# A decoder trunk on one core: how the mixer's GpSimd pieces of weights become a high and a low part

## The chip, the core and the metric

The kernel runs on one core of a Trainium2 chip. A core has five engines with a queue each: TensorE (PE in the profile, with its weight loads as PEld), VectorE (DVE), ScalarE (ACT), GpSimd (POOL) and SyncE (SP), which here only issues transfers. Sixteen DMA engines move the data, whichever queue issues them. The metric is the device time of one execution in microseconds (us). Three runs of the kernel before gave 1470.0, 1470.25 and 1474.0 us; the median is 1470.25.

## The reference

Two layers work on 256 tokens of 1024 features in float32. Each layer is a feed-forward block, a token mixer and a second feed-forward block, each with an RMS norm before and after it:

```
f = swiglu_ffn(rmsnorm(x, ffn1_norm_pre), ffn1_w_in, ffn1_w_out);  x = x + 0.5 * rmsnorm(f, ffn1_norm_post)
h = rmsnorm(x, mix_norm_pre);  p = h @ mix_w_in
qkv, z, beta_logit, a_logit, glu_in, gates = split(p)
y_a = gated_deltanet(qkv, z, beta_logit, a_logit, ...)      # causal convolution of 4 taps, delta rule in chunks
y_b = conformer_conv(glu_in, ...)                           # gated linear unit, causal convolution of 31 taps
g_a, g_b = split(sigmoid(gates));  y = (g_a * y_a + g_b * y_b) @ mix_w_out
x = x + rmsnorm(y, mix_norm_post)
f = swiglu_ffn(rmsnorm(x, ffn2_norm_pre), ffn2_w_in, ffn2_w_out);  x = x + 0.5 * rmsnorm(f, ffn2_norm_post)
```

The feed-forward blocks are 1024 x 5632 and 2816 x 1024 matrices; the mixer's input matrix is 1024 x 8208, and three of 1024 x 1024 follow it.

## The kernel before

All matrices are read once, in the order of use, as 444 pieces of 128 x 1024 float32 (512 KB; eight of them are 128 x 544). To keep float32 accuracy, each piece becomes two: a high part `hi`, the piece rounded to TensorE's float32r type, and a low part `lo`, exactly the rest. Activations are split in the same way, and a product is taken as three (`mm3`, lines 363 to 365): high x high, high x low, low x high.

`Stream` makes the pieces. `load_one` (lines 132 to 147) takes a raw buffer (three of them), and a high and a low buffer of a ring of `RING = 8` each. SP issues the load into the raw buffer (line 138), ScalarE copies it with rounding into `hi` (line 146), and VectorE or GpSimd subtracts `hi` from the raw piece into `lo` (line 147). `done()` is called when a piece's last product has been emitted; it emits the load of the next piece but seven, which can use the ring slot when TensorE has finished with it.

The list `side` says which engine subtracts: VectorE for all 66 + 66 pieces of the feed-forward blocks of a layer, GpSimd for the mixer's pieces 3, 16 to 63 and 67 out of 90 (`POOL`, line 64). With two layers that is 100 pieces for GpSimd and 344 for VectorE.

In the mixer, pieces 0 to 65 are the input matrix in 17 column chunks (`PLAN`), pieces 66 to 89 the three square matrices. A chunk's sums go into PSUM, are scaled by ScalarE (line 893), transposed by TensorE (line 509), and worked on by VectorE and ScalarE: convolutions of 4 taps (`c`, line 558) and of 31 taps (`cacc`, line 542), the decays of the delta rule (`decays`, lines 580 to 630), the inverses of 32 x 32 blocks (`iu`, lines 710 and 712, 31 steps of a product and a subtraction), and Newton steps for inverse square roots (`nw_a`, `nw_y`, lines 242 to 252).

The order of the work is set in two ways. On TensorE instructions are issued in the order in which the code emits them; `Lanes` puts transposes and small products between the big ones after a number of ticks written by hand (`DELAY`). On the other engines a planner orders the instructions by readiness in its own reckoning and by priority, which is program order with offsets (`CFG`). GpSimd has, beside the subtractions, one multiplication of `ktok` for each head group (line 666) and memsets of `u` (line 676) and `at` (line 744).

Of the kernel before, what the change touches and what calls it, by code (L numbers as in the profile page):

```python
# [9 lines left out]
F32 = mybir.dt.float32  # L10
# [3 lines left out]
ALU = mybir.AluOpType  # L14

P = 128
D = 1024
# [9 lines left out]

# columns of the per-channel parameter table
C_CW, C_DW, C_DB, C_BA, C_BG, C_LG, C_LB, C_NW = 0, 96, 344, 352, 360, 368, 376, 384
N_PCH = 385  # L30
# rows of the per-feature parameter table
R_F1PRE, R_F1POST, R_MPRE, R_MPOST, R_BO, R_F2PRE, R_F2POST = range(7)
# columns of the constants
K_ID, K_TRI, K_ONE, K_MASK = (128 * i for i in range(4))


# The mixer's column chunks in their order, each with the work that follows it; "f" takes its own sums.
PLAN = [
# [4 lines left out]
]  # L43
# Work between the products goes in steps: ticks (of three products) before each of them.
DELAY = {
# [7 lines left out]
}  # L53
# what has to be done before a piece of work starts
AFTER = {
# [6 lines left out]
}  # L62
# what has to be done when a chunk's sums are taken
BEFORE = {"z0": ("qt0",), "z1": ("qt1",), "b0": ("merge",), "b1": ("merge",), "a0": ("qt0",), "a1": ("qt1",)}
# the mixer's pieces whose split is GpSimd's
POOL = {3, *range(16, 64), 67}
# offsets of priority against program order
CFG = dict(stat=0, conv=-800, ev=1000, tok=4, st=4, post=300, pre=100, fin=None, tokens=200)


class Lanes:
    """Work in steps, between the products."""

# [43 lines left out]
class Stream:  # L117
    """Weights in the order of use: DRAM -> raw -> (hi, lo), hi + lo == raw exactly."""

# [12 lines left out]
    def load_one(self, parts=1):  # L132
        nc, src = self.nc, self.pieces[self.nload]
        n = src.shape[-1]
        raw = self.pool.tile([P, D], F32, name="raw", tag="raw", bufs=3)
        hi = self.pool.tile([P, D], F32R, name="whi", tag="whi", bufs=RING)
        lo = self.pool.tile([P, D], F32R, name="wlo", tag="wlo", bufs=RING)
        nc.sync.dma_start(raw[:, :n], src)
        eng = nc.gpsimd if self.side[self.nload] else nc.vector
        self.loaded.append((hi, lo))  # L140
        self.nload += 1
        for i in range(parts):
            if i:
                yield
            c = slice(i * n // parts, (i + 1) * n // parts)
            nc.scalar.copy(hi[:, c], raw[:, c])  # L146
            eng.tensor_tensor(lo[:, c], raw[:, c], hi.bitcast(F32)[:, c], op=ALU.subtract)  # L147

# [10 lines left out]
def trunk(ctx: ExitStack, tc: tile.TileContext, x_in, wfirst, consts, feat, pch, tokp,  # L159
# [35 lines left out]

    # ---- the residual stream and constants
    def xtile(tb):
# [39 lines left out]
    def rsqrt(o, v, n):  # L237
        """o = v ** -0.5 by a seed and Newton's steps."""
        y = work.tile([P, n], F32, name="nw_y", tag=f"nw_y{n}", bufs=2)
        a = work.tile([P, n], F32, name="nw_a", tag=f"nw_a{n}", bufs=2)  # L240
        hv = work.tile([P, n], F32, name="nw_h", tag=f"nw_h{n}", bufs=2)
        V.tensor_scalar(y.bitcast(I32), v.bitcast(I32), 1, None, op0=ALU.logical_shift_right)
        V.tensor_scalar(y.bitcast(I32), y.bitcast(I32), -1, 0x5F3759DF, op0=ALU.mult, op1=ALU.add)
        V.tensor_scalar(hv, v, -0.5, None, op0=ALU.mult)
        for it in range(3):
            dst = o if it == 2 else y
            if n == 1:
                V.scalar_tensor_tensor(a, y, y, hv, op0=ALU.mult, op1=ALU.mult)
            else:
                V.tensor_tensor(a, y, y, op=ALU.mult)  # L250
                V.tensor_tensor(a, a, hv, op=ALU.mult)
            V.scalar_tensor_tensor(dst, a, 1.5, y, op0=ALU.add, op1=ALU.mult)

    def split(hi, lo, src):
        """hi + lo == src"""
        S.copy(hi, src)
        V.tensor_tensor(lo, src, hi.bitcast(F32), op=ALU.subtract)  # L257
# [3 lines left out]

    # activations for the products: two tiles of four k-tiles, each with its high and its low parts
    def halves(tb):
        return [slots.tile([P, 2, 4, P], F32R, name="xt", tag=f"xt{tb}{hf}") for hf in range(2)]

    # ---- x * w, transposed and split; the rms of x goes into a per-token scale
    def pre(tb, wbc, xws):
# [24 lines left out]

    # ---- the same for the kernel's input, with w by channels, in step with the first pieces of the weights
    def start():
# [48 lines left out]

    # ---- x += half * rmsnorm(f) * w
    def post(tb, acc, wbc, half, fws, jks):
# [20 lines left out]

    # ---- h @ w for a list of chunks (columns, k-tiles of a piece); ev takes the sums, fin goes on
    def proj_in(xt, chunks, ev, fin, first=2):
# [34 lines left out]

    # ---- act @ w, all 1024 columns at once; the last 8 k-tiles one token block after the other
    def proj_out(lhs, nkt, ev, tails=0, need=None):
# [34 lines left out]

    # ---- feed-forward
    def ffn(xt, l, wpost, after, first=2, tails=0):
# [35 lines left out]

    # ---- token mixing
    def mixer(xt, l, after_mix):  # L480
# [22 lines left out]

        # -- staging of sums: scaled, transposed to channel-major, both token blocks side by side
        def to_channels(stage, cols):
# [5 lines left out]

        # ---- conformer module: gated linear unit
        hT = [slot(0, [P, 4, SEQ], name="hT0"), slot(1, [P, 4, SEQ], name="hT1")]
# [35 lines left out]

        # ---- delta rule  # L550
        ba = small(32, "ba", bufs=1).rearrange("p (k g b h) -> p k g b h", k=2, g=2, b=2)
# [17 lines left out]
        rq = small(16, "rq", bufs=1)  # L569
        ex = small(32, "ex", bufs=1)     # exp of: G | Gend - G  # L570
        neg_eg = small(16, "neg_eg", bufs=1)
# [61 lines left out]

        # sums over the channels of the squares, by tokens
        def squares(src, si):
# [85 lines left out]

        # the inverses of the 32-blocks on the diagonal, put together to 64 and to 128; the lower half of AT
        # and its diagonal blocks take what is in between
        def merge():
# [99 lines left out]

        # the first 128 tokens, from an empty state
        def scan_first():
# [15 lines left out]

        # the other 128
        def scan_second():
# [27 lines left out]

        # ---- the column chunks
        chunks = [{"ka": (272, 2), "kb": (256, 4)}.get(name, (512, 2)) for name, _ in PLAN]
# [175 lines left out]

        # gate[0..1]: tanh of g_a / 2; gate[2..3]: of g_b / 2; sigmoid = (tanh + 1) / 2
        def ev_b(tb, acc):
# [51 lines left out]

    # ---- layers
    xt = [None, None]
# [25 lines left out]
def _pieces(w, cols, kp):  # L1132
    """[L, K, N] -> [L, pieces, 128, kp * len(cols)], kp k-tiles to a piece"""
    s = w[:, :, cols]
    n_l, k, n = s.shape
    return s.reshape(n_l, k // (P * kp), kp, P, n).transpose(0, 1, 3, 2, 4).reshape(n_l, k // (P * kp), P, kp * n)
# [65 lines left out]
```

## Time and profile before

| | |
|---|---|
| time, median of 3 runs | 1470.25 us |
| span of the profiled execution | 1470.4 us |
| TensorE busy | 1395.6 us (95%) |
| VectorE busy | 1059.0 us (72%) |
| ScalarE busy | 769.5 us (52%) |
| GpSimd busy | 249.1 us (17%) |
| moved by DMA | 250.64 MB, mean 170 GB/s |
| mean granted clock of TensorE | 0.976 |

The profiled execution's span, from its first to its last instruction, stands for its time. The profile gives busy time by engine, by line and by stretch of the span. A row of a group reads: line, engine, operation, output <- inputs, shapes, count, then busy time and mean length in ns, then the idle time of the engine just before, and what ended it. A row of waits reads: engine and line, what it waited for, us in total, times, the longest. A row of a timeline reads: start, length, engine, line, operation. A row of DMA issues ends with the size of one and the median us from issue to landing. Neighbouring matmuls overlap, so their starts, not their lengths, give TensorE's pace. The first mixer lies between about 200 and 545 us, the second between about 930 and 1290.

### The profile page before, as it was taken

The numbers are of one execution on the slowest core, as the hardware profiler recorded it, in microseconds if no ns is written. First come the engines' busy times: TensorE is split into PE (matmuls) and PEld (weight loads), VectorE is DVE, ScalarE is ACT, GpSimd is POOL, SyncE is SP. The second block draws the span as 40 slices with busy tenths as digits, with TensorE's granted clock in tenths as the row PEclk, the third lists the DMA queues.
The fourth block names the chain that finished last, engine by engine and source line by source line (L and its number), as shares of the span: only waits on it lengthen the run. The fifth ranks groups of instructions, "written<-read, shape, count | busy, mean of one in ns | idle before, by whom it ended". The sixth has DMA issues, their size and how long they took to land.

```text
span 1470.4 us, 19499 instructions
## 1 busy us (share of the span) xinstructions
PE 1395.6 (95%) x6972; PEld 1154.8 (79%) x6972; DVE 1059.0 (72%) x2095; ACT 769.5 (52%) x1198; POOL 249.1 (17%) x116
## 2 busy tenths in 40 slices
PE   8999999886999999999999999996969999999997
PEld 6788878675778887888878888785758888788886
DVE  6655478899899877655486553898999997875543
ACT  7544357555555646544355443665555664464441
POOL 0000015445550000000000000173556300000000
PEclk9999999799999999999999999997989999999999
DMA  7766546343434556655466565553434435665551
GB/s 253 229 189 186 190 154 202 132 135 115 117 128 138 195 192 198 211 182 180 151 222 214 186 182 162 189 200 103 148 115 138 147 128 189 201 201 186 186 187 57
DMA packets 82962, 250.64 MB, mean 170 GB/s; under 512 B 21136, under 2 KB 21680, under 8 KB 82864
## 3 DMA queue, kind: packets, MB, share of 16 engines
q1 hardware_dynamic: 82576, 249.32, 52.3%
q8 instruction: 55, 0.90, 0.2%
q14 instruction: 43, 0.35, 0.1%
q10 hardware_dynamic: 288, 0.07, 0.0%
HBM read 245.14 MB, written 4.21 MB: 170 GB/s over the span
## 4 chain that ended last, share of the span: by engine, by line
PE 68%; DVE 20%; DMA 5%; ACT 4%; issue 2%; POOL 1%; DVEq 0%; ACTq 0%; POOLq 0%
PE mm L363 20%; PE mm L365 20%; PE mm L364 20%; DVE cacc L542 4%; DVE iu L712 2%; DVE c L558 2%; DVE iu L710 2%; DVE wlo L147 2%; DMA raw<-w1i 2%; ACT whi L146 2%; DMA raw<-mw 1%; PE tr L460 1%; PE gd L645 1%; DVE fw L352 1%; POOL wlo L147 1%
## 5 line engine op out<-in xcount | busy, mean ns | idle before, releaser
L146 ACT CAST whi<-raw 128x1024 fp32r<-128x1024 f32 (+2 forms) x445 | 462.8, 1041 | 382.7 <-PE mm L365 259.6
L147 DVE TENSOR_TENSOR wlo<-raw,whi 128x1024 fp32r<-128x1024 f32 (+2 forms) x345 | 417.3, 1212 | 272.3 <-ACT whi L146 265.3
L363 PE MATMUL mm<-whi,xt 128*128 128x512 f32 (+2 forms) x1280 | 515.9, 403 | 0.9 <-ACT whi L146 0.9
L365 PE MATMUL mm<-whi,xt 128*128 128x512 f32 (+2 forms) x1280 | 501.2, 392 | 3.8 <-DVE xt L257 3.6
L364 PE MATMUL mm<-wlo,xt 128*128 128x512 f32 (+2 forms) x1280 | 499.6, 390 | 0.5 <-DVE wlo L147 0.5
L365 PEld LDWEIGHTS mm<-whi,xt 128*128 128x128 f32 x1280 | 244.5, 191 | 60.1 <-DVE xt L257 7.5
L364 PEld LDWEIGHTS mm<-wlo,xt 128*128 128x128 f32 x1280 | 245.4, 192 | 45.3 <-DVE wlo L147 1.7
L363 PEld LDWEIGHTS mm<-whi,xt 128*128 128x128 f32 x1280 | 245.3, 192 | 45.2 <-ACT whi L146 1.3
L147 POOL TENSOR_TENSOR wlo<-raw,whi 128x1024 fp32r<-128x1024 f32 x100 | 239.7, 2410 | 236.4 <-ACT whi L146 228.1
L542 DVE SCALAR_TENSOR_TENSOR cacc<-hT,pc,cacc 128x254 f32<-128x254 f32 (+28 forms) x464 | 191.4, 462 | 4.9 <-ACT cacc L538 4.9
L363 PE MATMUL mm<-whi,act 128*128 128x512 f32 x352 | 137.6, 391 | 0.0
L365 PE MATMUL mm<-whi,act 128*128 128x512 f32 x352 | 137.1, 389 | 0.0
L364 PE MATMUL mm<-wlo,act 128*128 128x512 f32 x352 | 136.9, 389 | 0.0
L676 POOL MEMSET u<- 128x1024 f32 x4 | 3.8, 960 | 669.6 <-ACT jk L351 647.7
L365 PEld LDWEIGHTS mm<-whi,act 128*128 128x128 f32 x352 | 66.1, 188 | 13.9
L363 PEld LDWEIGHTS mm<-whi,act 128*128 128x128 f32 x352 | 66.1, 188 | 13.5
L364 PEld LDWEIGHTS mm<-wlo,act 128*128 128x128 f32 x352 | 66.1, 188 | 13.4
L448 ACT ACTIVATE ag<-mm,rstd 128x256 f32<-128x256 f32 x88 | 41.1, 474 | 56.8 <-DVE ag L449 23.9
L558 DVE SCALAR_TENSOR_TENSOR c<-tr,pc,c 128x255 f32<-128x255 f32 (+1 forms) x144 | 66.4, 473 | 2.0 <-ACT c L556 1.6
L449 DVE SCALAR_TENSOR_TENSOR ag<-mm,rstd,ag 128x256 f32<-128x256 f32 x88 | 41.6, 480 | 20.4 <-ACT ag L448 20.4
L556 ACT ACTIVATE c<-tr,pc 128x256 f32<-128x256 f32 x48 | 22.3, 472 | 54.6 <-DVE c L558 51.6
L352 DVE SCALAR_TENSOR_TENSOR fw<-mm,wbc 128x512 f32<-128x512 f32 x24 | 16.0, 687 | 46.2 <-ACT jk L351 46.2
(225 smaller groups left out, 1353.8 us busy)
## 6 DMA issues: line engine op xcount, KB each, us to landing
raw<-mw SPq DMA_DIRECT2D x168, 512.0 KB, 3.4
raw<-w1i SPq DMA_DIRECT2D x88, 512.0 KB, 4.0
raw<-w2i SPq DMA_DIRECT2D x88, 512.0 KB, 3.7
raw<-w1o SPq DMA_DIRECT2D x44, 512.0 KB, 3.6
raw<-w2o SPq DMA_DIRECT2D x44, 512.0 KB, 3.4
wbc<-feat SPq DMA_DIRECT2D x13, 512.0 KB, 4.6
raw<-mkb SPq DMA_DIRECT2D x8, 272.0 KB, 3.0
xs<-x SPq DMA_DIRECT2D x4, 512.0 KB, 3.6
```

Of the source, the lines that this page charges most:

```text
L146: nc.scalar.copy(hi[:, c], raw[:, c])
L147: eng.tensor_tensor(lo[:, c], raw[:, c], hi.bitcast(F32)[:, c], op=ALU.subtract)
L352: V.scalar_tensor_tensor(fw[:, cs], acc[hf], half, wbc[:, cs], op0=ALU.mult, op1=ALU.mult)
L363: T.matmul(o, xh, wh, start=start, stop=False)
L364: T.matmul(o, xh, wl, start=False, stop=False)
L365: T.matmul(o, xl, wh, start=False, stop=stop)
L448: S.activation(a[:, 0, :], ps[:, 0:256], AF.Silu, scale=xt[tb][1])
L449: V.scalar_tensor_tensor(a[:, 1, :], ps[:, 256:512], xt[tb][1], a[:, 0, :], op0=ALU.mult, op1=ALU.mult)
L542: cur = V.scalar_tensor_tensor(accs[i][:, sh:], h_of(t)[:, :SEQ - sh], dw(t, KW - 1 - sh), accs[i][:, sh:], op0=ALU.mult, op1=ALU.add)
L558: V.scalar_tensor_tensor(acc[:, sh:], src[:, :SEQ - sh], cw(t, 3 - sh), acc[:, sh:], op0=ALU.mult, op1=ALU.add)
L710: V.tensor_tensor(tmp, u[:, 0:n, s:s + 1].broadcast_to([P, n, m]), a[:, s:s + 1, s + 1:32].broadcast_to([P, n, m]), op=ALU.mult)
L712: V.tensor_tensor(u[:, 0:n, s + 1:32], u[:, 0:n, s + 1:32], tmp, op=ALU.subtract)
```

## The change

For the pieces that `side` gives to GpSimd, `load_one` now takes no raw buffer. GpSimd issues a DMA that reads the float32 piece from DRAM and writes it, cast to float32r, into `hi`. ScalarE multiplies `hi` by -1 into `lo`. GpSimd then issues a second DMA of the same piece from DRAM, which adds it to what stands in `lo`. GpSimd's subtraction is gone; the matrix piece is read twice. VectorE's pieces go as before, and so do the ring, the products and TensorE's order.

```diff
     def load_one(self, parts=1):
         nc, src = self.nc, self.pieces[self.nload]
         n = src.shape[-1]
-        raw = self.pool.tile([P, D], F32, name="raw", tag="raw", bufs=3)
         hi = self.pool.tile([P, D], F32R, name="whi", tag="whi", bufs=RING)
         lo = self.pool.tile([P, D], F32R, name="wlo", tag="wlo", bufs=RING)
-        nc.sync.dma_start(raw[:, :n], src)
-        eng = nc.gpsimd if self.side[self.nload] else nc.vector
+        by_dma = self.side[self.nload]
         self.loaded.append((hi, lo))
         self.nload += 1
+        if by_dma:
+            nc.gpsimd.dma_start(hi[:, :n], src)
+            nc.scalar.mul(lo[:, :n], hi.bitcast(F32)[:, :n], -1.0)
+            nc.gpsimd.dma_start(lo[:, :n], src, accum_op=ALU.add)
+            return
+        raw = self.pool.tile([P, D], F32, name="raw", tag="raw", bufs=3)
+        nc.sync.dma_start(raw[:, :n], src)
         for i in range(parts):
             if i:
                 yield
             c = slice(i * n // parts, (i + 1) * n // parts)
             nc.scalar.copy(hi[:, c], raw[:, c])
-            eng.tensor_tensor(lo[:, c], raw[:, c], hi.bitcast(F32)[:, c], op=ALU.subtract)
+            nc.vector.tensor_tensor(lo[:, c], raw[:, c], hi.bitcast(F32)[:, c], op=ALU.subtract)
```

## The prediction

> **What bounds the kernel now.** I read the page's busy times and its row of granted clock, then the busy times by stretches of 100 us, then the waits of TensorE, and last the groups and single instructions of VectorE and GpSimd in the first mixer.
>
> ```profile
> PE 1395.6 (95%) x6972; PEld 1154.8 (79%) x6972; DVE 1059.0 (72%) x2095; ACT 769.5 (52%) x1198; POOL 249.1 (17%) x116
> ...
> PEclk9999999799999999999999999997989999999999
> ...
> PE 68%; DVE 20%; DMA 5%; ACT 4%; issue 2%; POOL 1%; DVEq 0%; ACTq 0%; POOLq 0%
> ```
>
> ```profile
> 100.00:200.00 100.00, 100.00 (x453) 82.77 (x451) 51.71 (x63) 42.27 (x50) 2.16 (x2) 1.00 0.57 175
> 200.00:300.00 100.00, 86.13 (x450) 72.64 (x447) 84.85 (x231) 63.90 (x106) 41.83 (x20) 0.91 0.50 166
> 300.00:400.00 100.00, 86.35 (x410) 71.40 (x411) 91.75 (x220) 53.45 (x98) 53.59 (x23) 0.92 0.42 129
> ...
> 1000.00:1100.00 100.00, 78.89 (x366) 64.96 (x365) 94.27 (x238) 53.26 (x99) 51.11 (x23) 0.87 0.40 129
> ```
>
> The columns after the length are PE, PEld, DVE, ACT, POOL, granted clock, DMA share and GB/s. In the feed-forward (100 to 200) TensorE is full at clock 1.00. In the mixers it is not: 14 to 21 us of 100 idle, clock down to 0.87, VectorE at 85 to 94. What TensorE waits for there, over the whole run:
>
> ```profile
> PE tr L781 <- ACT vT L560: 17.9, 6, 5.7
> PE tr L509 <- DVE at L686: 10.8, 2, 5.8
> PE tr L509 <- ACT stg L893: 9.3, 7, 3.1
> PE gd L609 <- DVE g L605: 7.0, 2, 3.5
> ```
>
> Together 45.0 us, and none of it is a wait for weights: it is the mixer's own chain, which runs through VectorE. The idle time costs twice, since right after it the clock is low: at full clock the first of these rows (start, length) and the next but one start 0.45 us apart, 0.225 a product; behind a stall two neighbours of the chain of waits start 0.42 apart.
>
> ```profile
> 236.24 0.39 PE L364 MATMUL mm<-wlo,xt 128*128 128x512 f32 x1
> ...
> 236.69 0.39 PE L363 MATMUL mm<-whi,xt 128*128 128x512 f32 x1
> ```
>
> ```profile
> 279.33 0.43 PE mm L363
> 279.75 0.43 PE mm L364
> ```
>
> What the clock took in the three mixer stretches above: 0.09 x 86.1 + 0.08 x 86.4 + 0.13 x 78.9 = 24.9 us. So the most that any relief of the mixers can give is 45.0 + 24.9 = 70 us.
>
> VectorE is late in the mixers because of GpSimd. One subtraction of GpSimd takes 2.4 us, and VectorE's small instructions that start under one end only with it:
>
> ```profile
> L147 POOL TENSOR_TENSOR wlo<-raw,whi 128x1024 fp32r<-128x1024 f32 x100 | 239.7, 2410 | 236.4 <-ACT whi L146 228.1 <-ACT cacc L538 6.2 <-PE gd L732 1.4
> ```
>
> ```profile
> 331.75 7.06 POOL L147 TENSOR_TENSOR wlo<-raw,whi 128x1024 fp32r<-128x1024 f32 x3 [5.43 <-ACT whi L146]
> ```
>
> ```profile
> 331.99 2.28 DVE L710 TENSOR_TENSOR iu<-iu,ia 128x96 f32<-128x96 f32 x1
> ...
> 334.56 2.06 DVE L712 TENSOR_TENSOR iu<-iu 128x96 f32<-128x96 f32 x1
> ...
> 336.94 2.02 DVE L710 TENSOR_TENSOR iu<-iu,ia 128x115 f32<-128x115 f32 x1
> ...
> 339.27 0.26 DVE L712 TENSOR_TENSOR iu<-iu 128x115 f32<-128x115 f32 x1
> ```
>
> GpSimd's three subtractions run from 331.75 to 338.81; the three VectorE instructions under them take 2.0 to 2.3 us, and the next one of the same width, after them, 0.26.
>
> **The change part by part.** The sum is made against the profiled execution, a span of 1470.4 us; that is the runs' median (1470.25) but for 0.2 us, so no correction lies between.
>
> Removed are GpSimd's 100 subtractions, and with them what they hold VectorE up. These groups carry most of it:
>
> ```profile
> L712 DVE TENSOR_TENSOR iu<-iu 128x126 f32<-128x126 f32 (+22 forms) x62 | 40.8, 659 | 0.1
> L710 DVE TENSOR_TENSOR iu<-iu,ia 128x126 f32<-128x126 f32 (+22 forms) x62 | 37.4, 604 | 0.1
> L251 DVE TENSOR_TENSOR nw_a<-nw_a,nw_h 128x8 f32<-128x8 f32 (+1 forms) x30 | 19.2, 643 | 0.3
> L580 DVE TENSOR_TENSOR pre_a<-ba,tp 128x16 f32<-128x16 f32 x2 | 4.7, 2328 | 0.0
> L252 DVE SCALAR_TENSOR_TENSOR rq<-nw_a,nw_y 128x16 f32<-128x16 f32 x2 | 4.3, 2170 | 0.0
> L605 DVE SCALAR_TENSOR_TENSOR g<-lm,aexp 128x16 f32<-128x16 f32 x2 | 4.2, 2110 | 0.0
> L595 DVE TENSOR_TENSOR ls<-ls 128x16 f32<-128x16 f32 x2 | 4.1, 2058 | 0.0
> L599 DVE SCALAR_TENSOR_TENSOR lp<-lp,ls 128x16 f32<-128x16 f32 x14 | 2.3, 163 | 0.0
> ```
>
> L710 and L712 take 78.2 us in 124 instructions; at the free 0.26 us they would take 32.2, so 46.0 are excess. L251 at the free 0.163 us of line 599 (same kind of width) would take 4.9: 14.3 excess. Lines 580, 252, 605 and 595 take 17.3 in 8 instructions against 1.3: 16.0. Together **76 us**, 38 for each mixer, against the 70 that TensorE can give back. These lines are on the chain that makes `g`, the inverse and `vT`, for which TensorE waits; but TensorE's order is fixed in ticks, and some of these waits have several causes. I take half of the ceiling, **35 us** of gain; the ends are 0 and 70.
>
> ScalarE's part is moved, not added: a copy 128x1024 becomes a multiplication by -1 of the same shape, at 1.04 us a piece (462.8 us for 445 pieces). What changes is what it waits for. The copy waits for a free ring slot, with its raw data landed before; the multiplication waits for a landing that itself cannot start before the slot is free.
>
> ```profile
> L146 ACT CAST whi<-raw 128x1024 fp32r<-128x1024 f32 (+2 forms) x445 | 462.8, 1041 | 382.7 <-PE mm L365 259.6
> ```
>
> Added are two transfers of 512 KB a piece, and their issue on GpSimd.
>
> ```profile
> raw<-mw SPq DMA_DIRECT2D x168, 512.0 KB, 3.4
> x<-xs SPq DMA_DIRECT2D x4, 512.0 KB, 5.9
> ```
>
> ```profile
> 212.54 0.33 SPq L487 DMA_DIRECT2D xs<-x  x1
> ```
>
> A plain 512 KB (0.524 MB) lands 3.4 us after its issue. What it costs all 16 engines: in the stretch 100 to 200, 17.5 MB are 33.4 pieces and 57 us of engine time, 1.7 us each. For the casting one I take the same 1.7 and 3.4, since it moves the same bytes (its ends: 3.4, and the 5.9 of the slowest plain 512 KB). No row shows an accumulating transfer. Below it is a plain one, 1.7; above, three passes one after another (read the source, read what stands in the ring, write), 5.1. I take 2.5, nearer to the plain one, because the DRAM side is that of a plain one and the rest stays on the chip. So the engines have 4.2 us of work a piece. A DMA's issue on GpSimd is not in the trace either: between SP's 0.33 and the 2.4 of the subtraction it replaces; I take 0.7, twice SP's.
>
> What the pieces need: GpSimd's first and last low part of the run of 48 pieces (16 to 63) in the first mixer are
>
> ```profile
> 233.42 2.41 POOL L147 TENSOR_TENSOR wlo<-raw,whi 128x1024 fp32r<-128x1024 f32 x1 [19.90 <-ACT whi L146]
> ...
> 437.77 2.40 POOL L147 TENSOR_TENSOR wlo<-raw,whi 128x1024 fp32r<-128x1024 f32 x1 [0.48 <-ACT whi L146]
> ```
>
> 204 us for 47 steps, 4.35 us a piece. At full clock a piece costs TensorE 12 x 0.225 = 2.7 us, so the ring's 7 other pieces cover 19 us. The new way from free slot to low part is 0.7 + 3.4 + 1.04 + 0.7 + 3.4 = 9.2 us where nothing is in its way: covered, with about 10 us to spare. If that cover is gone, each us of it is a us of TensorE.
>
> Now GpSimd's queue. An accumulating DMA waits there for ScalarE's multiplication, and behind it stand the next casting DMA, the four multiplications of `ktok` (L666) and the memsets of the merge (L744). The planner orders GpSimd by when work comes ready in its own reckoning, so I expect casting DMA i+1 ahead of accumulating DMA i: a slot comes free every 2.7 to 4.35 us, a low part is ready for its sum 3.4 + 1.04 later. Then from one accumulating DMA to the next but one: issue 0.7, the transfer of the former 2.5, landing 3.4, ScalarE 1.04, issue 0.7, sum 8.3, 4.2 us a piece. That is under 4.35, and just enough for half the relief (204 - 17.5 over 47 steps is 4.0, plus the 10 us to spare over 47, 0.2). What stands behind a waiting DMA comes late by up to 3.4 + 1.04 = 4.4 us: 4 multiplications and 4 memsets, half of them on TensorE's path, 17.6, and rounding down for those that find the queue empty, **15 us** of loss. SP's queue only loses 100 loads and the raw buffers' waits on GpSimd; piece 3 starts when its slot is free instead of behind another raw buffer. Both count as nothing: SP has SP's idle time as cover, and without it the price is one landing, 3.4 us, per mixer.
>
> Sum: -35 + 15 = -20: **1450 us**.
>
> One rule of the Trainium skill speaks against this. Collectives: The Full Stack, section "The bandwidth ceiling: the fold count and why AG ≠ RS ≠ AR", says that a reduction in the DMA engines isn't slowed by the addition but by its two source reads, which halve the rate. No row here can show it. By it the accumulating transfer would be twice 1.7, 3.4 us, and the sum would go as in the first rival.
>
> **The rivals.** *The transfers become the bound.* If the accumulating transfer costs two plain ones one after another, 3.4, the engines have 5.1 us of work a piece: 47 x 5.1 = 240 us where 204 are needed now, less the 10 to spare, +26 a mixer, and VectorE's relief is swallowed: 1470 + 52 = 1522. At three passes, 6.8 a piece: 47 x 6.8 = 320, +106 a mixer, 1682. It decides from (204 + 10) / 47 = 4.55 us a piece on. For it: twice the reads; against it: a DMA share of 0.40 to 0.50 in the mixers today, which leaves room for one more plain pass. Chance 0.26.
>
> *GpSimd's queue goes in pairs.* If the planner puts cast, sum, cast, sum, the next casting DMA stands behind a wait for ScalarE: 0.7 + 3.4 + 1.04 + 0.7 = 5.8 us a piece at least, 47 x 5.8 = 273, +59 a mixer: 1590, and more where the landing stands behind the former sum's transfer. For it: that is the order in which the code emits them. Against it: VectorE's row above shows `iu` work put between other chains by readiness. Chance 0.15.
>
> *Nothing is gained.* GpSimd may hold VectorE up while it issues DMAs too, or TensorE's fixed order may not use the relief: 1470, up to 1485 with the 15 of loss. SBUF — State Buffer, section "Who interferes with whom", has VectorE with two SBUF inputs held up by a GpSimd instruction that reads, not by one that only writes; the rows above agree for the reading case (2.0 to 2.3 against 0.26 us), and by it the relief would be whole. Chance 0.13, two thirds of it within 0.3%. That the landing doesn't round, so that the low part is nearly zero, would change no time.
>
> **How the numbers follow.** The forecast has 0.46, with a range of its own from 1400 (the whole ceiling of 70) to 1465. So: faster 0.46; within 0.3% (4.4 us, about what a measurement of this kernel tells from no change) 0.09; slower 0.26 + 0.15 + 0.04 = 0.45. Both signs hold much of the chance, so the range takes in both: from 1400, below which nothing but a wrong ceiling lies, to 1600, which holds the first rival up to about 4.2 us an accumulating transfer and half the second; about 0.15 stays outside.
>
> **What would show it.** In the changed profile: the groups L710 and L712 near 0.26 us in the mean, L251 near 0.16; TensorE's waits in the mixers without `wlo` and `whi`, and a clock near 1.00 there; the DMA share of the mixers near 0.8. Wrong, if TensorE waits for `wlo` from a DMA, if the DMA share of the mixer is at its full height with fewer pieces in 100 us (first rival), or if GpSimd's queue waits for ScalarE on every piece with the DMA engines half idle (second). ScalarE's queue waiting several us for each landing, with `c` and `vT` late behind it, would be a cost that I have counted only in the 15.

## The result and the profile after

The changed kernel takes 1536.1 us (median of 4, 1534.8 to 1540.6) where the kernel before took 1472.1 beside it on the same chip: a ratio of 1.043, with an interval from 1.040 to 1.046. It is slower by 64 us; the forecast was 20 us faster. Line numbers of the mixer and of the helpers moved by five: 710 and 712 are now 715 and 717, 251 is 256, 509 is 514, 893 is 898. The ring's own lines are now 141 (casting DMA), 142 (multiplication by -1), 143 (accumulating DMA), 151 (copy) and 152 (VectorE's subtraction).

First the page of the changed kernel: its busy times, the rows of granted clock and DMA share, the queue that carries GpSimd's transfers, and the shares of the chain.

```profile
PE 1428.0 (93%) x6972; PEld 1177.9 (77%) x6972; DVE 961.8 (63%) x2095; ACT 769.0 (50%) x1198; POOL 151.3 (10%) x216
...
PEclk9999999798889999999999999998989899999999
DMA  7765558999996456655466655599999955566551
...
q0 software_dynamic: 28800, 104.87, 29.3%
...
PE 61%; issue 16%; DMA 10%; POOL 6%; DVE 4%; ACT 3%; POOLq 0%; DVEq 0%; ACTq 0%; SPq 0%
```

VectorE has 97 us less to do (1059.0 before), and the span is nevertheless longer. The DMA row stands at its full height in both mixers. In the chain, DMA and GpSimd have grown from 6% to 16%, and VectorE has gone from 20% to 4%: the end is no longer set where it was. "issue", time in which the engine waited for nothing that the profile shows, has grown from 2% to 16%; what stands behind it isn't told by the profile. The 100 pairs of transfers took 29.3% of 1533.9 us on all engines, which is 4.49 us a pair.

The busy times of the changed kernel by stretches (columns as in the prediction: PE, PEld, DVE, ACT, POOL, clock, DMA share, GB/s):

```profile
200.00:300.00 100.00, 84.67 (x410) 70.50 (x408) 60.03 (x181) 57.44 (x98) 21.31 (x30) 0.86 0.84 221
300.00:400.00 100.00, 80.11 (x359) 65.59 (x359) 67.82 (x233) 53.48 (x97) 32.89 (x45) 0.88 0.97 231
...
1000.00:1100.00 100.00, 80.58 (x409) 68.37 (x408) 64.00 (x220) 50.24 (x80) 31.48 (x44) 0.88 0.99 235
```

In the stretch 300 to 400 TensorE ran 359 instructions where it ran 410 before; its clock is 0.88 where it was 0.92, and the DMA engines are at 0.97 where they were at 0.42. VectorE fell from 92% to 68%, so it is not what holds TensorE back.

The groups of the changed kernel that answer to the prediction's rows:

```profile
L142 ACT ACTIVATE wlo<-whi 128x1024 fp32r<-128x1024 f32 x100 | 105.2, 1056 | 178.4 <-DMA whi<-mw 171.4
L143 POOL DMA_DIRECT2D wlo<-mw x96 | 83.7, 883 | 276.3 <-ACT wlo L142 224.0
L141 POOL DMA_DIRECT2D whi<-mw x96 | 69.5, 792 | 86.3 <-PE mm L370 77.7
...
L715 DVE TENSOR_TENSOR iu<-iu,ia 128x126 f32<-128x126 f32 (+22 forms) x62 | 15.3, 246 | 2.4 <-DMA ia<-dA 2.4
L717 DVE TENSOR_TENSOR iu<-iu 128x126 f32<-128x126 f32 (+22 forms) x62 | 15.2, 246 | 0.1
...
L256 DVE TENSOR_TENSOR nw_a<-nw_a,nw_h 128x8 f32<-128x8 f32 (+1 forms) x30 | 5.9, 202 | 0.2
```

VectorE's relief came as worked out: 604 and 659 ns became 246 each. Line 256 went from 643 to 202, where 163 was taken. What is new is in the first row: ahead of its 100 multiplications ScalarE stood idle for 178 us, 171 of them for the landing of the casting DMA. The issue view of the changed kernel (median from issue to landing) says how late that landing is:

```profile
gx<-gd SPq DMA_DIRECT2D x4, 512.0 KB, 8.4
...
whi<-mw POOLq DMA_DIRECT2D x96, 512.0 KB, 7.5
wlo<-mw POOLq DMA_DIRECT2D x96, 512.0 KB, 6.8
```

And the waits of the changed kernel (total, times, longest) show what this does:

```profile
ACT wlo L142 <- DMA whi<-mw: 171.4, 69, 8.5
...
DVE c L563 <- ACT c L561: 65.1, 27, 5.5
...
PE tr L514 <- ACT stg L898: 28.6, 12, 5.4
...
PE mm L369 <- DMA wlo<-mw: 2.4, 2, 1.7
```

TensorE waits almost never for a low part (2.4 us). It waits for ScalarE's `stg`, the scaled output of the products that it has to transpose: 28.6 us, where it was 9.3 before. VectorE waits for ScalarE's `c`: 65.1 us, where it was 1.6. One such place, in the timelines of ScalarE and then of TensorE:

```profile
263.82 1.06 ACT L142 ACTIVATE wlo<-whi 128x1024 fp32r<-128x1024 f32 x1 [4.43 <-DMA whi<-mw]
264.79 0.82 ACT L898 ACTIVATE stg<-mm,rstd 128x256 f32<-128x256 f32 x2
```

```profile
261.94 0.40 PE L370 MATMUL mm<-whi,xt 128*128 128x512 f32 x1
265.30 1.27 PE L514 MATMUL tr<-cst,stg 128*128 128x128 f32 x4 [2.96 <-ACT stg L898]
```

TensorE's last product ended at 262.34 (261.94 + 0.40), but `stg` starts only at 264.79: the multiplication stands ahead of it in ScalarE's queue and waits 4.43 us for its landing. TensorE, whose own order is fixed, stands for 2.96 us in front of the transposes.

GpSimd's timeline in the first mixer, the start of the run of 48 pieces and its end:

```profile
242.66 0.87 POOL L143 DMA_DIRECT2D wlo<-mkc  x1 [4.54 <-ACT kT L565]
243.22 0.86 POOL L141 DMA_DIRECT2D whi<-mw  x1
244.59 0.87 POOL L143 DMA_DIRECT2D wlo<-mkc  x1 [0.51 <-DVE c L563]
245.14 1.40 POOL L141 DMA_DIRECT2D whi<-mw  x2
251.36 0.88 POOL L143 DMA_DIRECT2D wlo<-mw  x1 [4.82 <-ACT wlo L142]
...
467.74 0.87 POOL L143 DMA_DIRECT2D wlo<-mw  x1 [5.27 <-ACT wlo L142]
```

Two and three casting DMAs go out ahead of the next accumulating one, so the queue doesn't go in pairs. From the first low part to the last it is 225.1 us for 47 steps, 4.79 us a piece (4.35 before). The pairs alone are 47 x 4.49 = 211 us of those 225.

### The profile page after: what moved, and what is told of

The parts are those of the page before. It is cut to its first block, busy times and chain, and to the rows that moved or that the text cites. A ratio compares the mean times of both kernels' runs of the same rounds, so it can differ in the third digit from the quotient of the medians.

```text
span 1533.9 us, 19499 instructions
## 1 busy us (share of the span) xinstructions
PE 1428.0 (93%) x6972; PEld 1177.9 (77%) x6972; DVE 961.8 (63%) x2095; ACT 769.0 (50%) x1198; POOL 151.3 (10%) x216
## 3 DMA queue, kind: packets, MB, share of 16 engines
q1 hardware_dynamic: 68176, 196.88, 40.5%
q0 software_dynamic: 28800, 104.87, 29.3%
## 4 chain that ended last, share of the span: by engine, by line
PE 61%; issue 16%; DMA 10%; POOL 6%; DVE 4%; ACT 3%; POOLq 0%; DVEq 0%; ACTq 0%; SPq 0%
PE mm L370 19%; PE mm L368 19%; PE mm L369 19%; DMA whi<-mw 5%; POOL wlo L143 3%; POOL whi L141 3%; DMA raw<-w1i 2%; DVE wlo L152 2%; PE tr L465 1%; ACT whi L151 1%; DVE fw L357 1%; ACT wlo L142 1%; DMA raw<-w2i 1%; DMA gx<-gd 0%; DMA whi<-mkc 0%
## 5 line engine op out<-in xcount | busy, mean ns | idle before, releaser
L368 PE MATMUL mm<-whi,xt 128*128 128x512 f32 (+2 forms) x1280 | 524.8, 410 | 6.3 <-ACT xt L261 4.1
L151 ACT CAST whi<-raw 128x1024 fp32r<-128x1024 f32 (+2 forms) x345 | 358.7, 1040 | 333.7 <-PE mm L370 238.0
L370 PE MATMUL mm<-whi,xt 128*128 128x512 f32 (+2 forms) x1280 | 508.6, 397 | 5.2 <-DVE ss L360 3.7
L369 PE MATMUL mm<-wlo,xt 128*128 128x512 f32 (+2 forms) x1280 | 507.6, 397 | 2.5 <-DMA wlo<-mw 2.4
L370 PEld LDWEIGHTS mm<-whi,xt 128*128 128x128 f32 x1280 | 249.3, 195 | 62.3 <-DVE ss L360 5.8
L368 PEld LDWEIGHTS mm<-whi,xt 128*128 128x128 f32 x1280 | 250.8, 196 | 52.8 <-ACT xt L261 4.6
L369 PEld LDWEIGHTS mm<-wlo,xt 128*128 128x128 f32 x1280 | 250.4, 196 | 49.7 <-DMA wlo<-mw 3.0
L142 ACT ACTIVATE wlo<-whi 128x1024 fp32r<-128x1024 f32 x100 | 105.2, 1056 | 178.4 <-DMA whi<-mw 171.4
L143 POOL DMA_DIRECT2D wlo<-mw x96 | 83.7, 883 | 276.3 <-ACT wlo L142 224.0
L563 DVE SCALAR_TENSOR_TENSOR c<-tr,pc,c 128x255 f32<-128x255 f32 (+2 forms) x144 | 67.4, 477 | 65.3 <-ACT c L561 65.1
L141 POOL DMA_DIRECT2D whi<-mw x96 | 69.5, 792 | 86.3 <-PE mm L370 77.7
L453 ACT ACTIVATE ag<-mm,rstd 128x256 f32<-128x256 f32 x88 | 41.0, 475 | 55.4 <-DVE ag L454 23.9
L514 PE MATMUL tr<-cst,stg 128*128 128x128 f32 x160 | 31.0, 316 | 38.6 <-ACT stg L898 28.6
```

Of the source, the lines that this page charges most:

```text
L141: nc.gpsimd.dma_start(hi[:, :n], src)
L142: nc.scalar.mul(lo[:, :n], hi.bitcast(F32)[:, :n], -1.0)
L143: nc.gpsimd.dma_start(lo[:, :n], src, accum_op=ALU.add)
L368: T.matmul(o, xh, wh, start=start, stop=False)
L369: T.matmul(o, xh, wl, start=False, stop=False)
L370: T.matmul(o, xl, wh, start=False, stop=stop)
```

## The experiments

Two causes stand against each other. **Theory A:** the DMA engines are full in the mixer. **Theory B:** ScalarE's in-order queue stands at the multiplication until the cast has landed. In short, with each ratio against the kernel before, run beside it (1471.8 to 1473.0 us, and 1476.4 beside late3, twothirds and onethird):

| kernel | us | ratio (95%) |
|---|---|---|
| changed | 1536.1 | 1.043 (1.040 to 1.046) |
| nosecond: no second transfer | 1427.0 | 0.969 (0.967 to 0.972) |
| nosum: second transfer without the addition | 1464.1 | 0.994 (0.993 to 0.995) |
| rawacc: raw load and copy as before | 1503.0 | 1.021 (1.019 to 1.023) |
| late: multiplication two pieces later | 1503.2 | 1.023 (1.016 to 1.029) |
| late3: three pieces later | 1501.1 | 1.017 (1.015 to 1.020) |
| half: every second piece by DMAs | 1498.9 | 1.018 (1.016 to 1.020) |
| halfrawpool: half, with raw loads | 1463.2 | 0.993 (0.991 to 0.995) |
| halflate: half, two pieces later | 1453.4 | 0.987 (0.984 to 0.990) |
| twothirds: two of three, later | 1459.5 | 0.988 (0.983 to 0.992) |
| onethird: one of three, later | 1482.0 | 1.007 (1.004 to 1.009) |
| negdve: VectorE negates | 1576.8 | 1.070 (1.069 to 1.072) |
| rawaccdve: raw loads, VectorE negates | 1549.6 | 1.052 (1.050 to 1.054) |
| alldve: VectorE subtracts all | 1521.4 | 1.033 (1.031 to 1.035) |
| negpool: GpSimd negates | 1640.0 | 1.114 (1.112 to 1.116) |

### Without the sum, and without the second transfer

`nosum` leaves out the addition, so its low part is not the rest of the piece:

```diff
-            nc.gpsimd.dma_start(lo[:, :n], src, accum_op=ALU.add)
+            nc.gpsimd.dma_start(lo[:, :n], src)
```

> The second DMA writes its cast piece into the low part instead of adding it (the sum is left out, so the low part is the high part again); queues, waits and bytes from DRAM stay. Theory A, the DMA engines are full because the accumulating transfer takes more engine time than a plain one: a pair falls from 4.5 us of 16 engines to about 3.4, the DMA share of the mixers from 0.97 to 0.75-0.85, the time to 1450-1490. Theory B, ScalarE's queue is what is late, standing at the multiplication until a cast piece lands: the engines' relief shortens the landing only from 7.5 to 5-6 us, time 1500-1530.

`nosecond` leaves the second transfer out altogether; its low part stays the negated high part:

```diff
-            nc.gpsimd.dma_start(lo[:, :n], src, accum_op=ALU.add)
```

> The second DMA is taken away (the low part is left as minus the high part). Theory A: 1.7 us of engine time a piece, DMA share of the mixers 0.40-0.50 as before the change, VectorE free of GpSimd's subtractions: 1400-1440. Theory B: the cast lands about 4.4 us after its issue and ScalarE still waits for it at each of 100 pieces: 1460-1510, ScalarE's wait for the landing above 100 us in total.

`nosum` came to 1464.1, `nosecond` to 1427.0. The queue of GpSimd's transfers, from the page of nosum and then of nosecond:

```profile
q0 software_dynamic: 28800, 104.87, 22.5%
```

```profile
q0 software_dynamic: 14400, 52.44, 12.2%
```

12.2% of nosecond's span of 1420.9 us is 1.73 us for one casting transfer; 22.5% of nosum's 1461.9 is 3.29 for the two, 1.56 for the second, which casts as the first does. Against the changed kernel's 4.49 the accumulating transfer costs 4.49 - 1.73 = 2.76 us. Landing and stretches of nosecond:

```profile
whi<-mw POOLq DMA_DIRECT2D x96, 512.0 KB, 3.6
```

```profile
300.00:400.00 100.00, 99.58 (x650) 82.27 (x649) 78.90 (x258) 66.94 (x125) 14.87 (x29) 0.98 0.52 152
1000.00:1100.00 100.00, 99.29 (x650) 82.55 (x649) 80.04 (x259) 68.04 (x130) 15.39 (x30) 1.00 0.55 160
```

So the relief of VectorE is real: without the second transfer TensorE is full, its clock is 0.98 to 1.00, and the time is 45 us under the 1472 of before. ScalarE waits for the landing of 3.6 us there too (the row below), and yet TensorE's wait for `stg` is 0.7 us in all:

```profile
ACT wlo L142 <- DMA whi<-mw: 66.8, 55, 4.9
```

The loss of the changed kernel is 1536 - 1427 = 109 us, and it comes with the second transfer: 37 us with its being there at all (1427 to 1464), 72 more with its being an accumulating one. Both times lie in the ranges written for theory A, and theory B's were missed; ScalarE's wait for the cast, over 100 us in nosecond by theory B, was 66.8 (73.9 in nosum). But theory B isn't out: the second transfer fills the engines, and it also makes the landing of the first late (3.6, 5.0 and 7.5 us in nosecond, nosum and the changed kernel), and with the last ScalarE's wait rises to 171.

### Half of the pieces

```diff
-        by_dma = self.side[self.nload]
+        side = self.side[self.nload]
+        by_dma = side and self.nload % 2 == 0
...
-            nc.vector.tensor_tensor(lo[:, c], raw[:, c], hi.bitcast(F32)[:, c], op=ALU.subtract)
+            eng = nc.gpsimd if side else nc.vector
+            eng.tensor_tensor(lo[:, c], raw[:, c], hi.bitcast(F32)[:, c], op=ALU.subtract)
```

> Every second of GpSimd's pieces goes by the two DMAs, the others by GpSimd's subtraction as before. Theory A: engine time a piece (4.5 + 1.65) / 2 = 3.1 us on the mean, under the 4.35 that the mixers need, so the engines don't bound and half of VectorE's relief counts: 1450-1475. Theory B: half of the waits in ScalarE's queue: about half of the loss, 1490-1515.

It took 1498.9, as theory B expected. A stretch of half and its waits:

```profile
300.00:400.00 100.00, 86.10 (x388) 69.73 (x387) 86.02 (x243) 52.42 (x97) 42.13 (x33) 0.88 0.72 182
```

```profile
ACT wlo L143 <- DMA whi<-mw: 97.1, 32, 5.9
...
PE tr L516 <- ACT stg L900: 32.2, 14, 7.0
```

At a DMA share of 0.72 the kernel is still 27 us slower than before, and TensorE's wait for `stg` is as long as in the changed kernel. Full engines can't be the whole of it.

### Raw loads as before, the sum by DMA

```diff
-            nc.gpsimd.dma_start(hi[:, :n], src)
+            raw = self.pool.tile([P, D], F32, name="raw", tag="raw", bufs=3)
+            nc.sync.dma_start(raw[:, :n], src)
+            nc.scalar.copy(hi[:, :n], raw[:, :n])
```

> GpSimd's pieces are loaded by SP into a raw buffer ahead of their slot and copied with rounding by ScalarE as before the change; ScalarE then multiplies by -1 and GpSimd's accumulating DMA adds the piece. Two reads from DRAM and the accumulating transfer stay, 1.65 + 2.76 = 4.4 us of engine time a piece against 4.49; what goes is ScalarE's wait for a landing that starts only when the slot is free; ScalarE gets 100 more instructions of 1.04 us. Theory A (full engines): 1520-1540. Theory B (ScalarE's queue stands until the landing): 1420-1455, the waits of TensorE for stg back under 10 us.

1503.0: between the two. The queue now holds the accumulating transfers alone, 18.3% of 1498.7 us in rawacc, 2.74 us each, which agrees with the 2.76 above:

```profile
q0 software_dynamic: 14400, 52.44, 18.3%
```

The load of the engines is nearly the same (0.95 and 0.96 over the 48 pieces of the two mixers, 0.98 and 0.97 in the changed kernel), the wait for the cast is gone, and 33 of the 64 us came back. TensorE's wait for `stg` is 6.2 us, under the 10 that theory B named, and the time is nevertheless far above theory B's range. The share isn't clean: this kernel gives ScalarE 100 more instructions, and ScalarE waits 40.5 us for the raw landings of these pieces (5.9 us in the median, 3.4 before).

### The multiplication later in ScalarE's queue

The next kernels change neither the transfers nor the arithmetic, only the place: the multiplication and its accumulating DMA are written later and tied to TensorE's last product of the second piece after the slot came free.

```diff
             nc.gpsimd.dma_start(hi[:, :n], src)
-            nc.scalar.mul(lo[:, :n], hi.bitcast(F32)[:, :n], -1.0)
-            nc.gpsimd.dma_start(lo[:, :n], src, accum_op=ALU.add)
+            self.due.append((self.nload, hi, lo, src, n))
+            if self.last is None:
+                self.late(None)
...
+    def late(self, after):
+        nc = self.nc
+        _, hi, lo, src, n = self.due.pop(0)
+        ins = nc.scalar.mul(lo[:, :n], hi.bitcast(F32)[:, :n], -1.0)
+        if after is not None:
+            self.tc.add_manual_dep(
+                ins.ins, after.ins.name,
...
+        nc.gpsimd.dma_start(lo[:, :n], src, accum_op=ALU.add)
...
+        while self.due and self.due[0][0] + 1 <= self.nload:
+            self.late(self.last)
...
-        T.matmul(o, xl, wh, start=False, stop=stop)
+        st.last = T.matmul(o, xl, wh, start=False, stop=stop)
```

> The changed kernel with the same two transfers a piece, but ScalarE's multiplication and the accumulating DMA behind it are made to come after the last product of the second piece that TensorE takes after the slot came free, so ScalarE's queue reaches the multiplication 5 to 9 us after the slot's release instead of at once. The output is complete. Theory A (the DMA engines are full: 4.49 us of their time a piece): nothing changes in their work, so the time stays at 1525 to 1540, with a DMA share near 0.97 and TensorE held back at the same pace of 4.5 to 4.8 us a piece. Theory B (ScalarE's queue stands at the multiplication until the cast has landed): ScalarE's waits for whi fall from 171 us to below 50, and the time to 1455 to 1490. If each is worth half, as the run with raw loads pointed to (33 of 64 us): about 1500.

> As the run named late (1503), but the multiplication and its accumulating DMA come one piece later still, after the third piece that TensorE takes. The output is complete. ScalarE still waited 97 us for whi in late. If those are what is left of the loss (theory B alone), the wait falls below 40 us and the time to 1470 to 1490. If what is left is the DMA engines' 4.49 us a piece (theory A), the wait falls and the time stays at 1495 to 1515; the low parts then come closer to their use, and TensorE may begin to wait for wlo from a DMA, with up to 1530.

late3 has `+ 2` for `+ 1`. They took 1503.2 and 1501.1. ScalarE's wait and one other of late3, then its small transfers:

```profile
ACT wlo L162 <- DMA whi<-mw: 39.7, 28, 2.8
...
ACT qT L579 <- DMA dU<-iu: 23.4, 2, 12.0
...
DVE iu L729 <- DMA ia<-dA: 23.0, 2, 17.6
```

```profile
dU<-iu SPq DMA_DIRECT2D x4, 128.0 KB, 18.2
```

```profile
gx<-gd SPq DMA_DIRECT2D x4, 512.0 KB, 5.0
...
dU<-iu SPq DMA_DIRECT2D x4, 128.0 KB, 3.4
```

The last fence is the issue view of the kernel before. The wait for the cast fell from 171 to 97 (late) and to 40 us (late3). The first step gave 33 us, the second nothing that can be told. GpSimd's own wait for ScalarE did not fall (225 us in the changed kernel, 215 in late, 235 in late3), so its queue isn't where the 33 us come from. TensorE's wait for `stg` went only from 28.6 to 23.9 and 13.5, so the whole way from ScalarE's queue to the time isn't shown.

What is left is the engines' own pace. The 48 pieces of the first mixer, in late and then in nosecond:

```profile
242.00:459.00 217.00, 185.21 (x1075) 154.90 (x1074) 142.79 (x474) 118.66 (x208) 68.32 (x96) 0.89 0.99 235
```

```profile
233.00:402.00 169.00, 166.69 (x1044) 141.37 (x1042) 138.28 (x459) 117.51 (x210) 27.84 (x52) 0.97 0.57 167
```

In late the engines are busy 0.99 of these 217 us, and 1.00 of 212 us in the second mixer; a pair takes 4.36 us of them (29.1% of 1497.4). nosecond gets through the same pieces in 169 us in either mixer, 3.6 us a piece, at a share of 0.57. A pair of 4.36 us can't come every 3.6 us, wherever the multiplication stands. Together the two stretches are 91 us longer in late, and 76 of these are left in the time (1503 - 1427). In the changed kernel the share over the 48 pieces is 0.98 and 0.97, over 225 and 226 us: it stands near the engines' limit too, and 13 of late's 33 us go with a pair's lower time (4.36 for 4.49); why that is lower isn't shown. Below the limit the price is open: nosum's two transfers need 3.29 us a piece, and its 48 pieces take 193 and 187 us at shares of 0.86 and 0.89, where nosecond's take 169.

So the place of the multiplication is worth about 35 us, and the other 74 of the 109 (1501 - 1427) stay with the second transfer. With the engines full, the mixer's own small transfers are late as well: in late3 the 128 KB of `dU`, 3.4 us before, land after 18.2, and VectorE's inverse and ScalarE's `qT` stand for them. How late such a transfer lands doesn't give its price, though: the gathers of `gx` land after 8.4 us in the changed kernel (5.0 before), but after 9.1 in nosum, which is 72 us faster.

### Half of the pieces, with the wait taken away

> Every second GpSimd piece goes by the two DMAs and the others by GpSimd's subtraction, as in the run named half (1499), and the multiplication is held back as in the run named late. The output is complete. The DMA engines were at 0.61 to 0.75 there, so theory A has no part in that run's 27 us over before. Theory B: the loss was ScalarE's wait for the landing (97 us); with it gone, half of the relief is left, 1473 - 22 = 1451, range 1440 to 1470. If the loss in half came from elsewhere (GpSimd's queue, where the subtractions stand behind DMAs that wait), it stays at 1485 to 1505.

> Every second GpSimd piece: raw load by SP's queue, ScalarE's copy and its multiplication by -1, accumulating DMA of GpSimd; the others by GpSimd's subtraction. The output is complete. No instruction of ScalarE waits for a transfer that starts only when the slot is free. Theory B: 1450 to 1470 (before less half of the relief of 45, plus up to 10 for 50 more instructions of 1.04 us on ScalarE). If the loss in half (1499) came from GpSimd's queue, where a subtraction stands behind a DMA that waits for ScalarE, it stays here: 1480 to 1505. Theory A gives nothing here beyond the share staying under 0.8.

halflate (the diffs of half and late together) took 1453.4, halfrawpool (half and rawacc together) 1463.2, both as theory B expected: with engines that aren't full, the loss of half goes when ScalarE no longer stands for the cast. The 48 pieces took 216 and 217 us in half, at DMA shares of 0.73 and 0.72, and 189 and 191 us in halflate, at 0.82 and 0.81: the engines carried more and were no bar. Waits of halflate:

```profile
ACT wlo L164 <- DMA whi<-mw: 18.9, 11, 4.0
...
PE tr L530 <- ACT stg L914: 11.3, 9, 2.7
...
POOL wlo L169 <- ACT wlo L164: 22.6, 16, 4.2
```

ScalarE's wait fell from 97 to 19 us and TensorE's wait for `stg` from 32 to 11. The last row is a caveat: GpSimd's own wait for ScalarE fell too, and the subtractions of the odd pieces stand behind it. In half this group was

```profile
L144 POOL DMA_DIRECT2D wlo<-mw x46 | 41.3, 897 | 159.6 <-ACT wlo L143 119.3
```

halfrawpool tells the two apart to some degree. GpSimd still waits for ScalarE there,

```profile
POOL wlo L146 <- ACT wlo L145: 83.5, 28, 7.6
```

and 36 of the 45 us are gained all the same. halflate computes the whole output and beats the kernel before by 1.3% (1.0 to 1.6%).

### Other shares

> As the run named halflate (1453), but two of three GpSimd pieces go by the two DMAs and one by GpSimd's subtraction. The output is complete. By the engine time of a piece, 2/3 of 4.49 and 1/3 of 1.7 are 3.6 us where halflate has 3.1 and late 4.49, against the 4.35 that a piece took before. Theory A with its edge at the full engines: VectorE's relief of two thirds of 45 us is still whole, 1472 - 30 = 1442, range 1435 to 1452. If the DMA engines cost time well before they are full, it lies between halflate and late: 1460 to 1480.

> As the run named halflate (1453), but one of three GpSimd pieces goes by the two DMAs. The output is complete. The DMA engines have 2.6 us a piece. Relief of one third of 45 us: 1472 - 15 = 1457, range 1450 to 1465. If the transfers cost time already in halflate, less of them gives at least as much: 1445 to 1453.

onethird gives the DMAs those pieces whose number 3 divides (34 of 100), twothirds the others. twothirds, 1459.5, is level with halflate (0.988 and 0.987, with overlapping intervals). Read by the ratio it lies between the two ranges written down for it: a larger relief of VectorE is there and is paid for elsewhere. ScalarE still waits 47 us for the cast in it, and the DMA share reaches 0.94 in one stretch; which of the two pays, isn't settled. onethird missed its range: 1482, 0.7% slower than before. Its inverse:

```profile
L733 DVE TENSOR_TENSOR iu<-iu 128x126 f32<-128x126 f32 (+22 forms) x62 | 38.4, 620 | 0.0
L731 DVE TENSOR_TENSOR iu<-iu,ia 128x126 f32<-128x126 f32 (+22 forms) x62 | 27.6, 445 | 0.0
```

The two lines together take 66.0 us, where they took 78.2 before, 55.3 in halflate, 45.3 in twothirds and 30.5 in the changed kernel. So VectorE's relief is there, a quarter of the whole with a third of the pieces, and it isn't what is missing. TensorE waits 12.0 us for low parts from the DMA in onethird; why just there, these runs don't tell. The planner orders the instructions of each kernel anew, and what that alone does to these times isn't separated.

### Another engine in ScalarE's place

```diff
-            nc.scalar.mul(lo[:, :n], hi.bitcast(F32)[:, :n], -1.0)
+            nc.gpsimd.tensor_scalar(lo[:, :n], hi.bitcast(F32)[:, :n], -1.0, None, op0=ALU.mult)
```

> GpSimd multiplies by -1 instead of ScalarE, so that only GpSimd's own queue stands until a cast piece lands; everything is still computed. Theory A: the engines stay full in the mixers (share 0.95 and up), TensorE now waits for low parts, 1530 or more. Theory B: ScalarE is free, its waits for whi<-mw are gone, 1450-1500; VectorE gets back at most 100 x 1.1 us of contention with GpSimd's reads.

> The changed kernel with VectorE instead of ScalarE multiplying by -1: VectorE's queue now stands until a cast piece lands, ScalarE's doesn't. Theory A: 1530-1545, as the engines are as full as before. Theory B, in the form that a queue which stands is what costs: ScalarE's waits for whi<-mw go, VectorE's come in their place; VectorE carries the chains of the mixer, so 1540-1600.

> As the run with raw buffers and the accumulating DMA, but VectorE multiplies by -1, so ScalarE has its instructions of before the change. Theory A: 1520-1540 again. Theory B: 1420-1460; against the run with ScalarE's multiplication it tells whether ScalarE's extra 100 us or VectorE's is cheaper.

negpool took 1640.0, outside theory B's range and in theory A's open one (1530 or more). But the run tells the theories apart badly, because GpSimd's queue is the bound, and TensorE waits 144.1 us for low parts. GpSimd's group:

```profile
L142 POOL TENSOR_SCALAR wlo<-whi 128x1024 fp32r<-128x1024 f32 x100 | 292.6, 2949 | 227.4 <-DMA whi<-mw 216.6
```

The wait for the landing (217 us), the negation (2.95 us each) and both issues stand one after another in one queue, which is the rival of the pairs after all, made by another engine. negdve (VectorE's `tensor_scalar` in the same line) took 1576.8, in theory B's range, and rawaccdve (the same behind raw loads) 1549.6, in neither: in the first VectorE's queue stands for the landing as ScalarE's did (111 us in 47 waits), in the second it takes 100 negations of 0.69 us on the engine that the change had relieved.

`alldve` has no DMA sums and no GpSimd at all:

```diff
-        by_dma = self.side[self.nload]
+        by_dma = False
```

> VectorE subtracts for all pieces: no GpSimd subtraction, no GpSimd DMA, one read of each piece. VectorE gets 100 x 1.22 = 122 us and loses the hold-ups of about 92 us. If VectorE's hold-ups are worth what the run without the second DMA gained (45 us) and 122 us of work cost as much for each us, the time is 1480 to 1490; it shows what GpSimd's help is worth in all.

1521.4, past the 1480 to 1490 that were expected. Its longest wait of TensorE is for `hT` (the transposes of line 975), 77.2 us in two waits, one at the end of each mixer: VectorE's convolution is put off until the pieces are done and is then late by 38.6 us. So VectorE has no room for these pieces either.

## Why the prediction was wrong

**Right.** VectorE's relief, its place and its cause: lines 715 and 717 at 246 ns where 260 were taken. Of the ceiling of 70 us I took half, 35; nosecond shows 45. (The ceiling counted TensorE's four longest waits, 45.0 us; the stretches from 200 to 500 and from 900 to 1200 have 57 us of idle time, so it was somewhat low, which decides nothing here.) The accumulating transfer costs 2.76 us where 2.5 were taken, the casting one 1.73 for 1.7, the issues 0.79 and 0.88 for 0.7. GpSimd's queue doesn't go in pairs, though its pace of 4.2 us a piece came out as 4.79.

**The step that failed** is the loss, the term of 15 us. It was made of 4.4 us for each of four of the eight instructions behind a waiting DMA on GpSimd, and those 4.4 were a landing of 3.4 us and one multiplication. Three things around that step don't hold, and the third touches the gain as well:

1. *The landing.* 3.4 us was the median of SP's plain loads in the kernel before. The cast alone does land after 3.6, but behind accumulating transfers it takes 7.5. The way from the slot to the low part is 0.79 + 7.5 + 1.06 + 0.88 + 6.8 = 17.0 us where I had 9.2. The ring's 19 us covered even that (2.4 us of waits for `wlo`), so the cover that I had checked held and was the wrong place to look.
2. *The queue.* I counted what stands behind the wait on GpSimd. The wait that costs is ScalarE's, which has `stg`, `c` and `cacc` behind it, with TensorE in turn behind `stg`. The prediction named this at its end as a cost counted only in the 15; by late and late3 it is about 35 us, and with half of the pieces, where the engines aren't full, 36 to 45 (halfrawpool and halflate against half).
3. *The engines.* I set the pair's 4.2 us against the 4.35 of before and concluded that it fits. The pair took 4.49, still under the 4.55 from which my first rival was to decide. By my own working that already leaves only 204 - (47 x 4.49 - 10) = 3 us of gain a mixer. And the mark itself was wrong: once VectorE is relieved, the pieces could come every 3.6 us (nosecond), and against that the pair is too long by 0.9 us, 47 times in each mixer, an estimate of 84 us in all. This is the larger part of the loss, about 74 us.

Put together: 1472 - 45 + 74 + 35 = 1536. These are the steps from before to nosecond, to late3, to the changed kernel, so that they add up is no proof, and the split between the last two isn't clean. In late3 the low parts also come later (TensorE waits 14.8 us for `wlo`), which makes the 74 too large; and a pair takes less of the engines there than in the changed kernel (28.5% of 1500.6 us, 4.28), which makes the 35 too large.

**The rivals.** The first, transfers as the bound, was right in kind, and its sign, a DMA share at full height, came. That it is near in time (1522) is in part luck: it took a price that was not paid (twice the casting transfer would have been 3.46 us, and 2.76 were measured), and it left out ScalarE's queue. The rule of the Trainium skill behind it (Collectives: The Full Stack, section "The bandwidth ceiling: the fold count and why AG ≠ RS ≠ AR") is stated there for the ReduceScatter of a ring; for this transfer the runs agree in its direction, 1.6 times the casting transfer, not in its factor of two. The second, pairs, didn't come: GpSimd's queue does wait for ScalarE, 225 us in 68 waits, but with the engines full, not half idle. The third, nothing gained, is refuted by nosecond. The rule named beside it (the Trainium skill, SBUF — State Buffer, section "Who interferes with whom") held: with GpSimd only issuing DMAs, VectorE's small instructions are at 246 ns.

**The signs that I had named.** Lines 715 and 717, and TensorE without waits for `wlo`, came as for a gain; the clock near 1.00 did not (0.86 to 0.88), and the DMA share was 0.84 to 0.99 in the stretches shown, where 0.8 was named. The last sign, ScalarE standing several us for each landing, was there in 69 of 100.

## What to carry to other kernels

An instruction that waits for a transfer costs what stands behind it in its engine's queue, so price a move from "data landed long before" to "data that lands now" by that queue, and with the landing as it is under the new load, not by the slack of the buffer it fills. Set the engines' time for a piece against the pace that the kernel would have after the change (3.6 us here), not against its pace of before (4.35): where the engines are the longer, as in late with a share of 0.99, no order of the queues helps. Half of a relief can be worth more than all of it: here every second piece by DMA, with the multiplication placed later, gave 1453 us, where all of them gave 1536.

## What the runs showed of the hardware

- An accumulating DMA of 512 KB from DRAM onto SBUF took 2.74 to 2.76 us of all 16 engines (rawacc; changed kernel less nosecond) where a casting one took 1.73 (nosecond). Its issue on GpSimd took 0.88 us in the mean (changed kernel), where those of nosum's two transfers took 0.54 and 0.53.
- A casting transfer that lands after 3.6 us (nosecond) takes 7.5 among accumulating ones (changed kernel), and 128 KB on SP's queue went from 3.4 to 18.2 us (before and late3) at DMA shares of 0.94 and 1.00 over the 48 pieces.
- GpSimd's multiplication of one 128x1024 input by a constant took 2.95 us (negpool), longer than its subtraction of two such inputs, 2.41 (before).
- VectorE's relief grows about with the pieces taken from GpSimd: the inverse's two lines took 78.2 us before, and 66.0, 55.3, 45.3 and 30.5 with 34 (onethird), 48 (halflate), 66 (twothirds) and all 100 (changed kernel) of them gone.
